# A first tile loaded in three column parts, with the parameter rows between the first and the second part

## The chip, the cores and the metric

The kernel runs on one core of one Trainium2 chip. The metric is the device time of one execution in microseconds. Ratios between kernels are the mean time of one kernel's fast runs over that of the other's fast runs of the same rounds, so they are not quite the ratio of the medians quoted beside them.

## The reference

Batch normalisation with fixed statistics over x of 32 x 256 x 128 x 128 float32:

```python
eps = 1e-5
return gamma * (x - mean) / np.sqrt(var + eps) + beta   # all four of length 256, along the channels
```

For each channel this is `x * scale + shift`. 537 MB go in and 537 MB come out; the four parameter vectors have 1 KB each.

## The kernel before

x is cut into 64 tiles of 128 partitions x 16384 columns (8.4 MB), which pass through three buffers. SP issues all loads, ACT all stores. VectorE computes columns 0 to 14335 of a tile in place, in two operations, and ScalarE the other 2048. The first tile is loaded in two halves, with the four parameter rows (each broadcast to 16 partitions) queued between them.

```python
left, right = slice(0, HW // 2), slice(HW // 2, HW)
nc.sync.dma_start(out=bufs[0][:, left], in_=xr[0][:, left]).then_inc(early, 16)
zeroed = step(nc.vector.memset(rows[:], 0.0))
for r, ap in enumerate((running_var, gamma, beta, running_mean)):
    inst = nc.sync.dma_start(out=rows[0:NE, r * C : (r + 1) * C], in_=ap.partition_broadcast(NE))
    if r == 0:
        inst._wait_ge(vec, zeroed)
    inst.then_inc(fetched, 16)
nc.sync.dma_start(out=bufs[0][:, right], in_=xr[0][:, right]).then_inc(loaded[0], 16)
for i in range(1, NT):
    s, turn = i % NBUF, i // NBUF
    if turn:
        nc.sync.wait_ge(stored[s], 16 * turn)              # the buffer is free
    inst = nc.sync.dma_start(out=bufs[s][:], in_=xr[i]).then_inc(loaded[s], 16)
    if turn:
        inst._wait_ge(vdone, 2 * (i - 1) + 1)              # VectorE is in the tile before
# ... cut: rows are transposed, scale and shift computed (VectorE, one square root on ScalarE)
vector_part(0, 0, HW // 2)._wait_ge(early, 16)
vector_part(0, HW // 2, VCOLS)._wait_ge(*landed(0))
# ... cut: vector_part for the other tiles, each waiting for landed(i)
for i in range(last):
    nc.scalar.wait_ge(vdone, 2 * (i + 1))
    inst = scalar_part(i, VCOLS)
    if i:
        inst._wait_ge(stored[(i - 1) % NBUF], 16 * ((i - 1) // NBUF + 1))
    store(i)                                               # waits for scalar_part(i)
```

## Time and profile before

| | before |
|---|---|
| median, first three runs | 2482.39 us (2482.02 to 2483.33) |
| span of the profiled run | 2483.3 us |
| bytes moved | 1073.85 MB, at a mean of 432 GB/s |
| VectorE, ScalarE busy | 20%, 6% |

The 16 DMA engines of this core are busy in all 40 slices of the profile (the prediction shows the line), at a mean of 432 GB/s. The prediction shows most of the lines. One more pair, from the timeline of the kernel before (start us, duration us, engine, line of the kernel, operation, idle time before with its releaser; SPq and ACTq in later lines are the issues of a DMA by SP and ACT):

```profile
74.26 2.09 ACT L141 ACTIVATE t<-t,shift_t,scale_t 128x2048 f32<-128x2048 f32 x1 [44.80 <-DMA out_dram<-t]
88.78 7.94 DVE L130 TENSOR_SCALAR t<-t,scale_t,shift_t 128x2560 f32<-128x2560 f32 x2 [26.45 <-DMA t<-in_x_dram]
```

At 74.26 a store has landed and the store queue is empty for a moment; at 88.78 a load has landed and the load queue is. The two moments are 14.5 us apart, so each queue has the other to fill in for it. Below this distance is called the spacing of the two gaps.

### The profile page before, as it was taken

To read this page: it belongs to the slowest core of one execution; us is meant where nothing else is said; L and a number is where in the kernel's file an instruction comes from. 1 tells how busy PE (TensorE), PEld (TensorE's weight loads), DVE (VectorE), ACT (ScalarE), POOL (GpSimd) and SP (SyncE) were. 2 spreads that over 40 slices of the span, in tenths; PEclk is the share of its full clock that TensorE was granted. 3 is DMA by queue.
4 is the path that set the end of the run, shared out by engine and by line. 5 is a ranking of instruction groups with operands and counts; after the bars stand their busy time and mean duration, and the time that the engine had idled before them with its cause. 6 is when DMAs were issued, how large, how long until landed. Compare 5 with 4: busy or idle time off the path is not lost.

```text
span 2483.3 us, 516 instructions
## 1 busy us (share of the span) xinstructions
DVE 508.8 (20%) x139; ACT 139.8 (6%) x66; POOL 0.2 (0%) x4
## 2 busy tenths in 40 slices
DVE  3122121221212212122121221212212122121220
ACT  0000000000000000000000000000000000000001
POOL 0000000000000000000000000000000000000000
DMA  9999999999999999999999999999999999999999
GB/s 415 430 439 434 428 436 436 435 433 430 432 433 438 430 432 433 435 424 437 437 428 436 438 436 429 437 435 430 436 437 436 430 437 435 429 437 435 433 433 408
DMA packets 18708, 1073.85 MB, mean 432 GB/s; under 512 B 2128, under 2 KB 2192, under 8 KB 2192
## 3 DMA queue, kind: packets, MB, share of 16 engines
q1 hardware_dynamic: 9488, 536.94, 50.1%
q10 hardware_dynamic: 9216, 536.88, 49.9%
q14 instruction: 4, 0.03, 0.0%
HBM read 536.94 MB, written 536.87 MB: 432 GB/s over the span
## 4 chain that ended last, share of the span: by engine, by line
DMA 93%; DVE 4%; another core or an unknown queue 1%; ACT 0%; issue 0%; SPq 0%; DVEq 0%
DMA t<-in_x_dram 93%; DVE t L130 4%; ACT t L141 0%; SPq L91 0%; DVE rows L89 0%; SPq L95 0%; DVE eps_t L107 0%; DVEq L198 0%; SPq L70 0%
## 5 line engine op out<-in xcount | busy, mean ns | idle before, releaser
L130 DVE TENSOR_SCALAR t<-t,scale_t,shift_t 128x11776 f32<-128x11776 f32 (+2 forms) x128 | 505.3, 3989 | 1930.4 <-DMA t<-in_x_dram 1930.2
L141 ACT ACTIVATE t<-t,shift_t,scale_t 128x2048 f32<-128x2048 f32 x64 | 138.2, 2159 | 2299.3 <-DMA out_dram<-t 2276.6
L108 DVE STREAM_TRANSPOSE turned<-rows 32x1024 f32<-32x1024 f32 x1 | 1.2, 1233 | 12.5 <-DMA rows<-in_running_mean_dram 12.5
L115 ACT ACT_TABLE_LOAD x1 | 1.3, 1283 | 0.9 <-SPq L70 0.9
L89 DVE MEMSET rows<- 32x1024 f32 x1 | 0.9, 912 | 1.2 <-SPq L70 1.2
L115 ACT ACTIVATE std_t<-par,eps_t 128x2 f32<-128x2 f32 x1 | 0.3, 296 | 14.7 <-DVE par L113 14.7
L113 DVE COPY par<-turned 32x8 f32<-32x8 f32 x4 | 0.6, 161 | 0.1
L122 DVE RECIPROCAL rstd_t<-std_t 128x2 f32<-128x2 f32 x1 | 0.2, 166 | 0.4 <-ACT std_t L115 0.4
L125 DVE TENSOR_TENSOR shift_t<-par,ms_t 128x2 f32<-128x2 f32 x1 | 0.2, 161 | 0.0
L124 DVE TENSOR_TENSOR ms_t<-par,scale_t 128x2 f32<-128x2 f32 x1 | 0.2, 161 | 0.0
L123 DVE TENSOR_TENSOR scale_t<-par,rstd_t 128x2 f32<-128x2 f32 x1 | 0.2, 160 | 0.0
L187 POOL MEMSET const-bfloat16-1.0<- 128x1 bf16 x1 | 0.1, 101 | 0.0
L187 POOL MEMSET const-uint8-127<- 128x1 uint8 x1 | 0.1, 101 | 0.0
L187 POOL MEMSET const-float32-0.0<- 128x1 f32 x1 | 0.1, 98 | 0.2 <-issue 0.2
L187 POOL MEMSET const-float32-1.0<- 128x1 f32 x1 | 0.1, 98 | 0.0
L107 DVE MEMSET eps_t<- 128x1 f32 x1 | 0.1, 59 | 0.1
## 6 DMA issues: line engine op xcount, KB each, us to landing
t<-in_x_dram SPq DMA_DIRECT2D x2, 4096.0 KB, 16.5
out_dram<-t ACTq DMA_DIRECT2D x64, 36.5
t<-in_x_dram SPq DMA_DIRECT2D x63, 37.0
rows<-in_running_var_dram SPq DMA_DIRECT2D x1, 16.0 KB, 11.3
rows<-in_gamma_dram SPq DMA_DIRECT2D x1, 16.0 KB, 11.1
rows<-in_beta_dram SPq DMA_DIRECT2D x1, 16.0 KB, 10.9
rows<-in_running_mean_dram SPq DMA_DIRECT2D x1, 16.0 KB, 11.3
```

Of the source, the lines that this page charges most:

```text
L89: zeroed = step(nc.vector.memset(rows[:], 0.0))
L107: step(nc.vector.memset(eps_t[:], eps))
L108: step(nc.vector.transpose(out=turned[:], in_=rows[:]), fetched, 16 * NPAR)
L113: placed = step(nc.vector.tensor_copy(out=flat[q * B : (q + 1) * B], in_=blocks[:, :, q, 0]))
L115: nc.scalar.activation(out=std_t[:], in_=var_t, func=mybir.ActivationFunctionType.Sqrt, bias=eps_t[:], scale=1.0,)._wait_ge(vec, placed).t ...
L122: step(nc.vector.reciprocal(out=rstd_t[:], in_=std_t[:]), act, 1)
L123: step(nc.vector.tensor_mul(out=scale_t[:], in0=gamma_t, in1=rstd_t[:]))
L124: step(nc.vector.tensor_mul(out=ms_t[:], in0=mean_t, in1=scale_t[:]))
L125: ready = step(nc.vector.tensor_sub(out=shift_t[:], in0=beta_t, in1=ms_t[:]))
L130: return nc.vector.tensor_scalar(out=t[:, first:end], in0=t[:, first:end], scalar1=scale_t[:, cb : cb + 1], scalar2=shift_t[:, cb : cb + 1 ...
L141: return nc.scalar.activation(out=t[:, first:], in_=t[:, first:], func=mybir.ActivationFunctionType.Identity, bias=shift_t[:, cb : cb + 1] ...
L187: nc = _bacc.Bacc("TRN2", target_bir_lowering=False, num_devices=1)
```

## The change

The intent is to get the parameters, and so the first elementwise operation, earlier: the rows then stand behind 0.8 MB of x instead of 4.2 MB.

```diff
+AHEAD = 1536
...
-        left, right = slice(0, HW // 2), slice(HW // 2, HW)
+        ahead, left, right = slice(0, AHEAD), slice(AHEAD, HW // 2), slice(HW // 2, HW)
...
-        nc.sync.dma_start(out=bufs[0][:, left], in_=xr[0][:, left]).then_inc(early, 16)
+        nc.sync.dma_start(out=bufs[0][:, ahead], in_=xr[0][:, ahead]).then_inc(early, 16)
         (memset of rows, the four row transfers)
+        nc.sync.dma_start(out=bufs[0][:, left], in_=xr[0][:, left]).then_inc(early, 16)
         nc.sync.dma_start(out=bufs[0][:, right], in_=xr[0][:, right]).then_inc(loaded[0], 16)
...
-        vector_part(0, 0, HW // 2)._wait_ge(early, 16)
+        vector_part(0, 0, HW // 2)._wait_ge(early, 32)
```

## The prediction

> **What bounds the kernel now.** I read four views, in this order: the page's summary, the table of stretches, the timeline of the first 30 us, and the waits of the load queue.
>
> The page (engines' busy time, then the DMA line of the 40 slices with its totals, then the chain that ended last):
>
> ```profile
> DVE 508.8 (20%) x139; ACT 139.8 (6%) x66; POOL 0.2 (0%) x4
> ...
> DMA  9999999999999999999999999999999999999999
> ...
> DMA packets 18708, 1073.85 MB, mean 432 GB/s; under 512 B 2128, under 2 KB 2192, under 8 KB 2192
> ...
> DMA 93%; DVE 4%; another core or an unknown queue 1%; ACT 0%; issue 0%; SPq 0%; DVEq 0%
> ```
>
> No compute engine is above 20%, the 16 DMA engines are full in every slice, and 93% of the chain is loads. The table of stretches (us, busy DVE, ACT, POOL, clock, DMA share, GB/s) says whether "full" holds closely:
>
> ```profile
> 0.00:30.00 30.00, 11.52 (x13) 3.67 (x3) 0.20 (x4) 1.00 0.99 411
> 30.00:100.00 70.00, 15.87 (x4) 2.09 (x1) 0.00 (x0) 1.00 0.99 423
> 100.00:500.00 400.00, 79.36 (x20) 21.64 (x11) 0.00 (x0) 1.00 1.00 434
> 2000.00:2440.00 440.00, 87.29 (x22) 25.11 (x12) 0.00 (x0) 1.00 1.00 434
> 2440.00:2478.00 38.00, 5.27 (x2) 6.36 (x1) 0.00 (x0) 1.00 1.00 433
> ```
>
> From 100 us on it holds: 433 to 434 GB/s, also in the last stretch, where loads end and stores finish alone. At 434 GB/s the 1073.85 MB take 2474 us. The span is 2483.3, so everything that start, end and slow spots cost together is 9 us. Nothing in the first tile can be worth more than a part of that 9 us; 2% would be 50 us.
>
> The timeline of the start (start us, duration us, engine, line, operation, idle time before with its releaser):
>
> ```profile
> 0.95 0.38 SPq L88 DMA_DIRECT2D t<-in_x_dram  x1
> 2.15 0.34 SPq L91 DMA_DIRECT2D rows<-in_running_var_dram  x1
> ...
> 3.46 0.43 SPq L91 DMA_DIRECT2D rows<-in_running_mean_dram  x1
> 3.93 0.44 SPq L95 DMA_DIRECT2D t<-in_x_dram  x1
> ...
> 14.79 1.23 DVE L108 STREAM_TRANSPOSE turned<-rows 32x1024 f32<-32x1024 f32 x1 [12.54 <-DMA rows<-in_running_mean_dram]
> ...
> 18.04 4.55 DVE L130 TENSOR_SCALAR t<-t,scale_t,shift_t 128x8192 f32<-128x8192 f32 x1
> 23.85 3.48 DVE L130 TENSOR_SCALAR t<-t,scale_t,shift_t 128x6144 f32<-128x6144 f32 x1 [1.27 <-DMA t<-in_x_dram]
> 27.36 2.09 ACT L141 ACTIVATE t<-t,shift_t,scale_t 128x2048 f32<-128x2048 f32 x1 [10.23 <-DVE t L130]
> 29.49 0.37 ACTq L154 DMA_DIRECT2D out_dram<-t  x1
> ```
>
> The parameter rows stand behind 4 MB of x, so the transpose starts only at 14.79, and the first elementwise operation at 18.04 instead of at about 14.05, when its half of the tile had landed (0.95 plus 13.1 to landing, by that line's issues). That 4 us is what the change aims at. But it does not reach the first store: the second VectorE operation started at 23.85 after waiting 1.27 us for the right half. The store at 29.49 hangs on that landing, not on the parameters.
>
> The load queue's own waits (for what, total us, times, longest) show the rest of the run:
>
> ```profile
> SPq L101 <- DMA out_dram<-t: 1398.1, 61, 68.8
> SPq L102 <- DVE t L130: 985.0, 61, 16.2
> ```
>
> From the fourth tile on, a load waits for a store to free its buffer and for VectorE's first part of the tile before it. These gaps cost nothing while a store is in flight, which the 434 GB/s confirms.
>
> **What the Trainium skill says.** "DMA: Bandwidth & Descriptors", section "Where 436 GB/s comes from", gives a ceiling of 435 GB/s for 16 engines; the 434 measured here is that ceiling, so only bytes or idle time can change the run. The same page, "Queues, rings and completion order", says that each DMA engine takes the descriptors of a ring in order; the trace agrees: the last row, issued at 3.46, landed 11.3 us later, behind the 4 MB, and DVE starts on it at 14.79. "Latency and other measured facts" gives about 600 ns for the first byte of a transfer issued from SP; here the first x packets appear near 1.95 us in the DMA view of the first microseconds, 1.0 us after the issue's start and 0.6 after its end at 1.33. "Anatomy of one DMA" puts most of a transfer's fixed cost of 2 us into the receipt after the last byte. Here the row packets run from about 12.1 to 13.6 us and the last row lands at 14.76, so 1.2 us after.
>
> **The change part by part.** Bytes and compute instructions stay the same. The static order of instructions of the changed kernel confirms it: one more issue on SP, all else in place.
>
> Step 1, the parameters come earlier. The first part has 128 x 1536 x 4 B = 0.79 MB, 1.8 us at 434 GB/s. It starts at 1.95, takes about 0.6 us more to ramp up (my estimate from the first packets of before, which took 1.8 us where later ones of that size took 1.2), and is out of the way at about 4.4. The last row is still issued at 3.46, reaches the engines about 1.0 us later at 4.5, and lands at about 6.3. The transpose starts there instead of at 14.79, and the scale and shift are ready 18.04 - 14.79 = 3.25 us later, at 9.6 instead of 18.04. Saved on VectorE: 8.4 us.
>
> Step 2, the DMA engines run dry for a moment. Their queue holds 9.7 us of work (4.19 MB) while SP issues the rows in the kernel before; now it holds 1.8 us. The second part is issued where the right half was, at 3.93, and reaches the engines at about 5.0. Between 4.4 and 5.0 there are only 64 packets of 1 KB. So about 0.6 us are idle or nearly so, and a second ramp of about 0.6 us follows because nothing is in flight. Against this stands what the rows cost in the kernel before, where they also thinned the stream (my sum of the packets around 12 to 14 us gives about 0.3 us lost). Net loss: 0.6 + 0.6 - 0.3 = +0.9 us on the bounding resource.
>
> Step 3, one more issue and 128 more packets. The issue of 0.44 us moves the right half and the loads of tiles 1 and 2 later, but the 3.4 MB of the second part keep the engines busy for 7.9 us meanwhile: hidden. The extra packets are 8 for each engine; I put them below 0.1 us.
>
> Step 4, the first tile. The left half is complete at about 14.05 + 0.9 = 15.0; parameters are ready long before, so VectorE starts there, 3 us earlier than 18.04, and ends at 19.5. The right half lands at 23.85 + 0.9 = 24.7, and VectorE waits some 5 us for it instead of 1.27. The 3 us turn into a longer wait. The first store goes at about 29.49 + 0.9 = 30.4. No gain here.
>
> Step 5, from there the same schedule 0.9 us later. Loads 1 and 2 (16.8 MB, 39 us) are queued already, so even the store's moment does not leave the engines idle.
>
> Sum: -0 (VectorE's gain is hidden) + 0.9 + at most 0.1 = +0.8 to +1.0 us on 2482.39, so 2483.3 us.
>
> **Rivals.**
> (a) The earlier parameters pull the first store forward and some of it reaches the end. The 4 us idle of VectorE before 18.04 speak for it; the 1.27 us wait for the right half and the full DMA engines speak against it. If the whole 1.27 us and no dry spell came through, 2481.1.
> (b) The dry spell of step 2 does not occur, since row packets and the second part arrive quickly enough, or the row packets cost less near an empty queue. Then the change is nothing but noise: 2482.4.
> (c) A changed phase between loads and stores makes their gaps coincide, and the engines idle in every tile. In the timeline the gap of the loads (88.75 to 90.42) lies 13.8 us after that of the stores (74.26 to 76.38), and both repeat each 38.6 us. A shift below 1 us is far from a collision. If it did happen, about 2 us for each of 64 tiles would make it some 2610 us, 5% slower. I give it 0.5%.
>
> **Range and chances.** The mechanisms (a) to step 2 span 2481.1 to 2483.4. Three runs of the kernel before differ by 1.3 us, and another chip may shift the level by as much again. So 2481.0 to 2485.4 should hold it 8 times in 10. A gain of 50 us isn't possible with the same bytes at the ceiling; a loss of 50 us needs (c). Faster 0.4%, within 2% 99%, slower 0.6%.
>
> **What would show each step right or wrong.** Step 1: transpose at about 6.3 us, first elementwise operation no longer released by the parameters. Step 2: a visible hole in the DMA view between 4 and 6 us, and a landing of the right half some 0.9 us later than 23.83. Step 4: VectorE's wait before its second operation grows from 1.27 to about 5 us, first store at about 30.4. Step 5: 434 GB/s between 100 and 2440 us, load spacing still 38.6 us. I am wrong if the store goes before 29.0 us and the end comes earlier by as much, if no hole appears, or if any stretch after 100 us has another rate.

## The result

| | before | changed |
|---|---|---|
| median (range), six runs each | 2482.26 us (2482.02 to 2484.1) | 2483.98 us (2483.42 to 2487.24) |
| ratio to before, 95% interval | | 1.0009 (0.9996 to 1.0022) |
| profiled span | 2483.3 us | 2481.9 us |
| parameters' transpose starts | 14.79 us | 6.23 us |
| first store issued | 29.49 us | 30.16 us |

The timeline of the changed kernel's start, columns as above:

```profile
0.95 0.38 SPq L90 DMA_DIRECT2D t<-in_x_dram  x1
...
3.92 0.42 SPq L97 DMA_DIRECT2D t<-in_x_dram  x1
...
6.23 1.23 DVE L111 STREAM_TRANSPOSE turned<-rows 32x1024 f32<-32x1024 f32 x1 [3.99 <-DMA rows<-in_running_mean_dram]
...
14.81 4.55 DVE L133 TENSOR_SCALAR t<-t,scale_t,shift_t 128x8192 f32<-128x8192 f32 x1 [5.45 <-DMA t<-in_x_dram]
24.52 3.48 DVE L133 TENSOR_SCALAR t<-t,scale_t,shift_t 128x6144 f32<-128x6144 f32 x1 [5.16 <-DMA t<-in_x_dram]
...
30.16 0.37 ACTq L157 DMA_DIRECT2D out_dram<-t  x1
```

The parameters are 8.6 us earlier and the first elementwise operation 3.2 us, now released by x and not by the rows. Then all of it is gone: VectorE waits 5.16 us for the right half instead of 1.27, starts on it 0.67 us later than before, and the first store goes 0.67 us later.

What the DMA engines did meanwhile is in the DMA view of 1.5 to 6 us (40 slices of 0.11 us; a packet's bytes count in the slice in which it starts). Before, then changed:

```profile
GB/s 0 0 0 0 2039 1748 0 291 0 583 0 0 0 0 0 0 0 0 0 291 874 1748 874 291 291 0 291 0 0 0 291 874 1456 1456 291 0 0 291 0 0
```

```profile
GB/s 0 0 0 0 437 55 218 109 55 218 55 273 109 437 382 218 546 328 546 328 546 328 546 328 546 200 374 155 137 91 956 710 1183 237 237 0 0 473 0 0
```

Before, packets of 32 KB start in bunches and each keeps its engine busy for over 1 us, so zeros between them are no idle time. In the changed kernel the packets of the first part (6 KB) start densely until 4.3 us, then come five thin slices of 200, 374, 155, 137 and 91 GB/s with the rows in them, and the second part starts only at 4.9 us. That is the hole.

Its size can be counted from the trace. I take the bytes of the load queue's packets, each spread evenly over its recorded time, divide by 435 GB/s (the stretches after 100 us hold 433 to 435), and subtract that from the time since the first packet. The rest is the time the load stream has lost. The columns count from the first packet, which starts at 1.95 us, so "3 us" is 4.95 on the timeline:

| us lost by ... after the first packet | 3 us | 5 us | 8 us | 12 us | 20 us |
|---|---|---|---|---|---|
| before | 0.86 | 0.90 | 0.92 | 1.22 | 1.32 |
| changed | 1.04 | 1.84 | 1.99 | 2.05 | 2.08 |

Before, 0.86 us go at the ramp, where the first packets take 1.85 us in the median instead of 1.21 later, and 0.30 at the rows, between 8 and 12 us. A finer count places the loss of the changed kernel on the timeline: 0.79 us by 4.5 us (before 0.85), 1.08 by 5.0 (before 0.86) and 1.85 by 7.0 (before 0.90). So the hole itself costs some 0.3 us and lies before the 3 us column. The 0.8 us between the 3 us and the 5 us column are a second ramp: the engines have packets again, but the first of these take 1.50 us in the median, where later ones of the second part take 0.99. The difference at 20 us is 0.76 us.

From there on the same schedule runs. Three lines of the changed kernel's table of stretches (columns as in the prediction), and its chain by engine:

```profile
0.00:30.00 30.00, 11.53 (x13) 3.54 (x3) 0.20 (x4) 1.00 0.94 387
...
100.00:500.00 400.00, 79.35 (x20) 20.92 (x10) 0.00 (x0) 1.00 1.00 433
...
2000.00:2440.00 440.00, 87.29 (x22) 25.11 (x12) 0.00 (x0) 1.00 1.00 434
```

```profile
DMA 92%; DVE 4%; another core or an unknown queue 2%; ACT 0%; issue 0%; SPq 0%; DVEq 0%
```

The rate differs in the first 30 us, 387 GB/s instead of 411, and the next 70 have 430 instead of 423. Packets count here where they start, which blurs the edges of a stretch; over the 100 us it is 417 against 419. The same blur stands in the last stretch, 2440 to 2478 us, with 426 against 433. In between the bound is the same.

Why then is the profiled span of the changed kernel shorter, 2481.9 against 2483.3? The timelines of before, then of the changed kernel, at the first operation on a later tile:

```profile
591.16 7.94 DVE L130 TENSOR_SCALAR t<-t,scale_t,shift_t 128x2560 f32<-128x2560 f32 x2 [30.80 <-DMA t<-in_x_dram]
630.88 7.93 DVE L130 TENSOR_SCALAR t<-t,scale_t,shift_t 128x2560 f32<-128x2560 f32 x2 [31.78 <-DMA t<-in_x_dram]
...
2448.30 5.27 DVE L130 TENSOR_SCALAR t<-t,scale_t,shift_t 128x2560 f32<-128x2560 f32 x2 [30.70 <-DMA t<-in_x_dram]
```

```profile
89.50 7.93 DVE L133 TENSOR_SCALAR t<-t,scale_t,shift_t 128x2560 f32<-128x2560 f32 x2 [26.52 <-DMA t<-in_x_dram]
...
2446.87 5.27 DVE L133 TENSOR_SCALAR t<-t,scale_t,shift_t 128x2560 f32<-128x2560 f32 x2 [31.11 <-DMA t<-in_x_dram]
```

Tile 2 comes 0.72 us later in the changed kernel (89.50 against 88.78), the last tile 1.43 us earlier. In between a tile takes 38.64 us, but some take longer: 39.72 us from 591.16 to 630.88. In the profile of before four tiles exceed 38.75 us, 2.4 us together; in that of the changed kernel one, by 0.4. In a later profile of the changed kernel it was twenty tiles and 6.3 us. These long tiles come and go between executions of one program and are larger than what the change does. Between 100 and 2440 us the three profiles lose 4.8 (before), 1.8 (changed) and 7.1 us (the later one) against 434.5 GB/s, with the engines' idle time equal within 0.1 us, so the difference is in packets that take longer; why they do is open. It is of the size of the 5 us by which single executions here differ, and no ratio below is finer than about 0.12% either way.

### The profile page after: what moved, and what is told of

It is laid out like the page before. It is cut to its first block, busy times and chain, and to the rows that moved or that the text cites. A ratio compares the mean times of both kernels' runs of the same rounds, so it can differ in the third digit from the quotient of the medians.

```text
span 2481.9 us, 517 instructions
## 1 busy us (share of the span) xinstructions
DVE 508.8 (20%) x139; ACT 139.8 (6%) x66; POOL 0.2 (0%) x4
## 4 chain that ended last, share of the span: by engine, by line
DMA 92%; DVE 4%; another core or an unknown queue 2%; ACT 0%; issue 0%; SPq 0%; DVEq 0%
DMA t<-in_x_dram 92%; DVE t L133 4%; ACT t L144 0%; SPq L93 0%; DVE rows L91 0%; SPq L97 0%; DVE eps_t L110 0%; DVEq L201 0%; SPq L71 0%
```

## The experiments

Eleven experiments ran, two of which repeat a program; all gave the reference's result. Theory: the DMA engines are full, so the change costs the hole in the load stream and gains nothing. Rivals: the split itself costs the time; an earlier first store is worth something; what matters is how the gaps of the two queues lie to each other.

Many expectations name the landing of tile 1 as the mark of a hole. That was a bad mark: by then the first store shares the engines, and it shifts between 46.0 (late10) and 57.7 us (ahead512), while the load streams differ by 2 us at most at 20 us. By this mark several expectations failed: it came at 54.56 in again, which is the changed program that had shown 55.05, at 55.64 in ahead3072 and 55.62 in split_only (54.4 to 54.5 expected, and the rival's value was 55.0), at 57.66 in ahead512 (56.2) and 52.73 in rows_act (54.3 to 54.5). The mark was given up after these results; the loss of the load stream, counted as above, took its place:

| us lost by ... after the first packet | 3 us | 5 us | 8 us | 12 us | 20 us |
|---|---|---|---|---|---|
| again (the changed kernel) | 1.05 | 1.93 | 2.03 | 2.05 | 2.08 |
| ahead512 | 2.25 | 3.05 | 3.09 | 3.15 | 3.18 |
| ahead3072, ahead3072b | 0.95, 0.91 | 1.13, 1.08 | 1.53, 1.48 | 1.59, 1.54 | 1.63, 1.58 |
| split_only | 0.85 | 0.87 | 0.94 | 1.30 | 1.44 |
| rows_act | 0.84 | 0.88 | 1.12 | 1.65 | 1.82 |
| early_store, late5 (start as before) | 0.84, 0.76 | 0.88, 0.80 | 0.89, 0.81 | 1.22, 1.15 | 1.32, 1.24 |

The last row, with the 1.32 of the kernel before itself, says how far such a figure repeats: within about 0.1 us.

### again: the changed kernel once more

No edit.

> The changed kernel once more, byte for byte the same program, for more runs on one chip beside the kernel before. Theory (a dry spell of the DMA engines of about 0.7 us in the first tile, nothing else): tile 1 lands at 55.05 again (before 54.40), and the median is 0.7 us above the kernel before, give or take what sporadic long tiles add. Rival (the change also costs something later, as the medians 2483.98 against 2482.26 suggest, 1.7 us): the difference stays at 1.5 us or more while tile 1 lands 0.65 late.

Measured: 2485.78 us median (2483.44 to 2489.0), beside 2483.53 (2482.04 to 2486.11) for before; ratio 1.0008 (0.9996 to 1.0021). The loss of 2.08 us is that of the first profile. The medians differ by 1.7 us and 2.3 us in the two sets, where the hole explains 0.8, but both intervals include no difference: whether there is more stays open. The packets give one hint, told at the end.

### ahead3072 and ahead3072b: a first part twice as long

```diff
-AHEAD = 1536
+AHEAD = 3072
```

> First part 3072 columns (1.57 MB, 3.6 us at 434 GB/s) instead of 1536, all else as changed. Theory of the dry spell: the first part ends at about 6.2 us, after the second part has reached the engines at 5.0, so the hole is gone: right half 0.6 us earlier than in the changed kernel, tile 1 lands at 54.4 to 54.5, median within 0.3 of the kernel before; parameters ready at about 11.4. Rival (splitting the transfer or its smaller packets cost the time): as slow as the changed kernel, tile 1 at 55.0.

> The 3072 column version once more, same program, for a second profile of its start and five more times. Theory: loads short by 1.6 to 1.7 us of full rate by 20 us (before 1.33, changed kernel 2.09 in two profiles), and within 0.5 us of the kernel before in the median. If the short stretch at the first store (28 to 60 us: 0.12 us lost against 1.23 and 1.27 in the changed kernel) belongs to the start and not to chance, it is near 0.12 again.

Measured: 2482.75 us beside 2483.53, ratio 0.9996 (0.9983 to 1.0008); the second time 2485.07 beside 2484.5, ratio 1.0004 (0.9992 to 1.0017). The loss is 1.6 us, so 0.5 us of the 0.76 are back, not all: of the 0.8 us between 3 and 5 us only 0.2 are left, but 0.4 us go between 5 and 8, during and after the row packets (4.4 to 5.8 us in these columns). The first expectation (no hole, tile 1 as in before within 0.1) was too bold, the second held. The timeline of ahead3072:

```profile
8.88 1.23 DVE L111 STREAM_TRANSPOSE turned<-rows 32x1024 f32<-32x1024 f32 x1 [6.63 <-DMA rows<-in_running_mean_dram]
14.48 4.55 DVE L133 TENSOR_SCALAR t<-t,scale_t,shift_t 128x8192 f32<-128x8192 f32 x1 [2.47 <-DMA t<-in_x_dram]
```

The parameters are still ready well before x. So the aim of the change can be had for 0.3 us instead of 0.76, and is no use either way.

### ahead512: a first part a third as long

```diff
-AHEAD = 1536
+AHEAD = 512
```

> First part 512 columns (0.26 MB, 0.6 us of work) instead of 1536. Theory of the dry spell: the first part ends 1.2 us earlier and the second part still comes at 5.0, so the hole is 1.2 us longer: tile 1 lands at 56.2 (changed kernel 55.05), median 1.2 us above the changed kernel. Rival (split cost): the same as the changed kernel, 55.0, since parts and packets are as many.

Measured: the loss is 3.18 us, 1.10 above the changed kernel, where 1.2 was expected; the second operation on tile 0 starts 1.03 us later than in again:

```profile
25.32 3.48 DVE L133 TENSOR_SCALAR t<-t,scale_t,shift_t 128x6144 f32<-128x6144 f32 x1 [5.16 <-DMA t<-in_x_dram]
```

The median is 2486.03 us beside 2483.53, ratio 1.0012 (0.9998 to 1.0026); it is 0.25 us above that of again, where 1.2 was expected, but the noise is larger than both. With as many parts and packets the loss grew by what the shorter first part leaves uncovered. All of the growth stands at 3 us already (2.25 against 1.05), where the longer hole is; the second ramp, from 3 to 5 us, is 0.8 to 0.9 us in both. That speaks for the hole and against the split.

### split_only: the split alone

Both left parts go before the rows.

```diff
         nc.sync.dma_start(out=bufs[0][:, ahead], ...).then_inc(early, 16)
+        nc.sync.dma_start(out=bufs[0][:, left], ...).then_inc(early, 16)
         (the rows)
-        nc.sync.dma_start(out=bufs[0][:, left], ...).then_inc(early, 16)
```

> Three parts as in the change (1536, 6656 and 8192 columns), but both left parts issued before the parameter rows, so only the split is left of the change. Theory of the dry spell: no hole, since the second part is issued 0.4 us after the first: tile 1 lands at 54.4 to 54.5, parameters late as before (transpose at about 14.8), median within 0.3 of the kernel before. Rival (split cost): tile 1 at 55.0.

Measured: 2482.82 us beside 2483.53, ratio 0.9996 (0.9983 to 1.0008). The loss is 1.44 us, 0.12 above before.

```profile
14.35 1.23 DVE L111 STREAM_TRANSPOSE turned<-rows 32x1024 f32<-32x1024 f32 x1 [12.09 <-DMA rows<-in_running_mean_dram]
...
23.58 3.48 DVE L133 TENSOR_SCALAR t<-t,scale_t,shift_t 128x6144 f32<-128x6144 f32 x1 [1.45 <-DMA t<-in_x_dram]
```

The rows are late again and the right half is early again. The split costs about 0.1 us; the rest of the 0.76 comes from where the rows stand.

### rows_act: the rows in a queue of their own

```diff
-            inst = nc.sync.dma_start(out=rows[0:NE, ...
+            inst = nc.scalar.dma_start(out=rows[0:NE, ...
```

> The kernel before (two halves) with the four rows issued from ACT instead of SP, so they have a ring of their own and SP issues the right half at once. Theory: the rows no longer stand behind 4 MB, the transpose starts at about 6 to 7 us, and the x stream has no hole: tile 1 lands at 54.3 to 54.5, median within 0.3 of the kernel before. So the aim of the change is met without its cost, and is still worth nothing in time. Rival (early parameters are worth something once the hole is gone): 1 us or more faster than the kernel before.

Measured: 2483.78 us beside 2484.37, ratio 0.9997 (0.9985 to 1.001). The time is as expected, the reason fell. Two views of rows_act, its timeline and its DMA issues (last column: us to landing):

```profile
16.36 1.23 DVE L108 STREAM_TRANSPOSE turned<-rows 32x1024 f32<-32x1024 f32 x1 [14.10 <-DMA rows<-in_running_mean_dram]
```

```profile
rows<-in_running_var_dram ACTq DMA_DIRECT2D x1, 16.0 KB, 7.5
rows<-in_gamma_dram ACTq DMA_DIRECT2D x1, 16.0 KB, 9.6
rows<-in_beta_dram ACTq DMA_DIRECT2D x1, 16.0 KB, 10.9
rows<-in_running_mean_dram ACTq DMA_DIRECT2D x1, 16.0 KB, 12.7
```

The rows came later than from behind 4 MB (16.36 against 14.79). Issued 0.5 us apart, they land about 2.2 us apart. The Trainium skill, "DMA: Bandwidth & Descriptors", section "Queues, rings and completion order", says that each engine takes turns between rings, a packet at a time. That would give this: each row has a data packet and a semaphore packet on an engine, and if each waits for one x packet of 32 KB (1.22 us), the step is 2.4 us. The time agrees; the turns themselves I did not follow engine by engine. So early parameters without a hole were not tried by this run, and its rival was not tested by it.

### early_store: the first store sooner

```diff
-            nc.scalar.wait_ge(vdone, 2 * (i + 1))
+            nc.scalar.wait_ge(vdone, 2 * (i + 1) if i else 1)
             inst = scalar_part(i, VCOLS)
+            if i == 0:
+                inst._wait_ge(*landed(0))
+                nc.scalar.wait_ge(vdone, 2)
```

A first form of it, without the wait for one VectorE part, was found to read the shift too early.

> The kernel before with ACT's part of the first tile waiting for the right half and one finished VectorE part instead of both, so it runs beside VectorE and the first store goes at about 27.4 instead of 29.5. Theory (the engines are full, the first store's moment is worth nothing): median within 0.3 of the kernel before, tile 1 lands a little later (it shares earlier), the stores land earlier. Rival (an earlier first store comes out at the end): 2 us faster.

Measured: the store goes early, as its timeline shows:

```profile
27.05 0.37 ACTq L154 DMA_DIRECT2D out_dram<-t  x1
```

The median is 2485.17 us beside 2484.37, ratio 1.0006 (0.9992 to 1.0019). A gain of 2 us would be a ratio of 0.9992, the very end of the interval; the mean is 1.5 us the other way. So an earlier first store shows no gain.

### ahead3072_early: a try at beating both

The edits of ahead3072 and early_store together.

> A try at a version that beats both: first part 3072 columns, and ACT's part of the first tile beside VectorE's, so the first store goes at about 27.7. Theory (bytes at the ceiling, nothing to gain): within 0.5 us of the kernel before, give or take the sporadic long tiles. Rival (an earlier first store shows once the parameters are early): 1.5 to 2 us faster.

Measured: 2487.73 us (four runs, 2484.46 to 2493.16) beside 2484.5, ratio 1.0016 (1.0002 to 1.0029). It beats nothing, is not within the 0.5 us expected, and is slower if anything; from four runs, one of them at 2493, I draw no cause.

### late5, late10 and wait_tile1: the first store later

In the kernel before, four or eight more transposes of the rows (late5, late10), or one wait (wait_tile1):

```diff
         step(nc.vector.transpose(out=turned[:], in_=rows[:]), fetched, 16 * NPAR)
+        for _ in range(4):          # late10: 8
+            step(nc.vector.transpose(out=turned[:], in_=rows[:]))
```

```diff
+        nc.vector.wait_ge(*landed(1))
         vector_part(0, 0, HW // 2)._wait_ge(early, 16)
```

> The kernel before with four more transposes of the rows (each 1.23 us, result unchanged), which put off the parameters by about 5 us and the first store with them: 29.5 becomes about 33.2 (the wait of 1.27 us for the right half swallows a part). Theory: the loads of tiles 1 and 2 keep the engines full until 63 us, so the end is within 0.3 of the kernel before. Rival (the first store's moment counts): 3.7 us slower.

> The kernel before with the first elementwise operation waiting until tile 1 has landed (about 43.5 us with no store beside it), so the first store goes at about 54 us, 24 us late. Theory: the store then lands after the load queue is empty (63 us), tile 3's load and tile 1's store are released by the same landing, and their gaps coincide from there on: the engines run dry once in each tile. I expect 2 to 4 us for each tile, 2600 to 2730 us, a load spacing of 41 to 43 us and 380 to 410 GB/s. Rival (the two queues drift apart again, or the gaps are covered): at most some 10 us slower, spacing back at 38.64.

> As late5 with eight extra transposes instead of four, so the first store goes about 5 us later still, near 37.6. In the eight runs so far the time from a store's landing to the next load's landing settles at about 9.7, 14.5 or 19.3 us, steps of 4.84 us, which is two packets of 2.42 us; before and after have 14.5, late5 9.7, and wait_tile1 has the two 2.4 us apart the other way and lost 3.6 us in each tile. Theory (what counts is whether the two gaps coincide, not the first store's moment): a spacing of 4.84 us here, where the gaps nearly touch; if they just miss each other the time is within 5 us of the kernel before, if they touch 20 us or more above it, and unsteady from run to run, as the one run of late5 at 2595.82 hints. Rival (the first store's moment itself counts): 7 to 8 us slower, all of it before 100 us, with 434 GB/s afterwards.

| | first store issued | spacing: store's landing to next load's landing | median | ratio to before (95%) |
|---|---|---|---|---|
| before | 29.49 us | 14.5 us | 2484.37 us (beside late5, wait_tile1) | 1 |
| late5 | 32.62 us | 9.7 us | 2487.16 us with one run at 2595.82 (slow), 2486.91 without | 1.0009 (0.9996 to 1.0023) |
| late10 | 37.77 us | 2.4 to 5.1 us | 2602.93 us with one run at 2731.79 (slow), 2600.73 without | 1.047 (1.0455 to 1.0484) |
| wait_tile1 | 52.92 us | the store lands 2.4 us after the load | 2723.94 us | 1.0964 (1.0949 to 1.0979) |

The timelines of late5, late10 and wait_tile1, each with one store's landing (start of the ACT line) and one load's (start of the DVE line):

```profile
74.82 2.10 ACT L143 ACTIVATE t<-t,shift_t,scale_t 128x2048 f32<-128x2048 f32 x1 [42.23 <-DMA out_dram<-t]
...
84.54 7.94 DVE L132 TENSOR_SCALAR t<-t,scale_t,shift_t 128x2560 f32<-128x2560 f32 x2 [25.93 <-DMA t<-in_x_dram]
```

```profile
161.46 2.09 ACT L143 ACTIVATE t<-t,shift_t,scale_t 128x2048 f32<-128x2048 f32 x1 [38.81 <-DMA out_dram<-t]
...
166.34 7.94 DVE L132 TENSOR_SCALAR t<-t,scale_t,shift_t 128x2560 f32<-128x2560 f32 x2 [33.07 <-DMA t<-in_x_dram]
```

```profile
163.78 7.94 DVE L130 TENSOR_SCALAR t<-t,scale_t,shift_t 128x2560 f32<-128x2560 f32 x2 [34.22 <-DMA t<-in_x_dram]
166.20 2.10 ACT L141 ACTIVATE t<-t,shift_t,scale_t 128x2048 f32<-128x2048 f32 x1 [40.09 <-DMA out_dram<-t]
```

And a line each of the tables of stretches of late10 and wait_tile1 (the last two figures are DMA share and GB/s):

```profile
500.00:1000.00 500.00, 95.23 (x24) 25.11 (x12) 0.00 (x0) 1.00 0.99 411
```

```profile
500.00:1000.00 500.00, 95.22 (x24) 25.14 (x12) 0.00 (x0) 1.00 0.95 396
```

Of the other versions again, ahead512, rows_act and ahead3072b keep a spacing of 14.5 us, while ahead3072, split_only, early_store and ahead3072_early settle at 19.3; in both groups one queue has work while the other has its gap, and neither is faster beyond noise. Note that ahead3072 and ahead3072b are one program: the spacing can differ between executions.

Both wait_tile1 (2600 to 2730 us) and late10 (20 us or more if the gaps touch) came out as expected, and the rate falls in all of the run, not at the start. Counted over all packets like the loss above, the engines miss 129 us in late10 and 244 us in wait_tile1, against 6 to 12 us in all other profiles (here at 434.5 GB/s): 2.0 and 3.9 us for each of some 63 tiles. A first store 8 us late costs 116 us (2600.73 - 2484.5, fast runs), one 3 us late 2.5 us, if anything. So it is not the store's moment by itself that counts; the loss goes with the spacing. Where a gap of the loads (landing, VectorE's first part, issue, first packet) meets a gap of the stores (landing, ScalarE's part, issue, first packet), neither queue has work.

That is only a part of the loss, and in late10 the smaller one: its line above has a DMA share of 0.99 at 411 GB/s, so the engines are occupied and yet move less. Counted from the packets of the tiles 3 to 61, idle engines are 0.5 of the 2.0 us lost for each tile in late10, and 2.2 of 3.9 in wait_tile1. The rest passes with a packet on every engine, but packets that take longer: in late10, after its two gaps at 163 to 165 us, the rate is 308 to 341 GB/s from 172 to 178 us with all 16 engines occupied. A 64 KB packet takes 2.42 us in the median of all these profiles; the slowest twentieth takes over 3.2 us in late10 and wait_tile1, and in before 2.42 still holds for 95 of 100. In the 39 tiles of late10 with a spacing of about 4.8 us the engines idle for 0.03 us and 1.2 us are lost all the same; in the 20 with less, 1.5 of 3.5 us are idle time. Why packets take longer after gaps that meet or nearly meet is open.

In late5 I expected a time within 0.3 us; the medians differ by 2.5 us (fast runs), in an interval that includes none, so that stays undecided. Its run at 2595.82 lies at late10's level, and late10's at 2731.79 at that of wait_tile1. Both are called slow only because they are over 1.5% above the fastest run of their kernel; the recorded clock is 1.00 in them as in all others. They may be executions whose gaps settled closer together, but they left no trace, so that is not shown.

## Why the prediction was right

The 2483.98 us (2483.3 predicted) and the range held. The time alone proves little, since 2482.4 with no hole at all would have lain in the range too; what decides are the steps:

- **The bound.** Right for this change: 433 to 435 GB/s from 100 us to 2440 in both kernels, and no version got below the time of before by more than noise. Too narrow was "only bytes or idle time can change the run": in late10 most of the loss is in packets that take longer on occupied engines.
- **Step 1, parameters.** Right: transpose at 6.23 us for 6.3.
- **Step 2, the hole.** The mechanism is shown: it stands in the DMA view at 4.3 to 4.9 us, deepens by 1.10 us with a shorter first part, and goes with a longer one. The net size was 0.76 us for 0.9. Against before, on the timeline: 0.06 less lost by 4.5 us, 0.28 more in the hole (4.5 to 5.0), 0.73 in the second ramp (5.0 to 7.0), 0.12 up to 10 us, then 0.24 saved where the rows no longer stand and 0.07 after. The prediction had put 0.6 for the hole and 0.6 for the ramp. The first part ended at 4.73 us, not at 4.4, so the hole was half as long, and the ramp cost more. That their sum of 1.2 came near 1.07 is partly luck; the 0.3 for the rows was 0.31.
- **Step 3, split.** About 0.12 us in split_only, for "below 0.1".
- **Step 4, the first tile.** Right: VectorE at 14.81 us for 15.0, a wait of 5.16 for some 5, the store at 30.16 for 30.4.
- **Step 5.** 0.72 us late at tile 2. Later the long tiles, which I had not considered beyond the spread of three runs, hide it; the two sets of runs differ by 1.7 and 2.3 us with intervals that reach 0.
- **Rival (a)**, an earlier store: not in the change (the store went later), and when forced in early_store it brought nothing. **Rival (b)**, no hole: refuted by the packets, though the time alone would not have told it. **Rival (c)**, coinciding gaps: rightly excluded for this change, since the spacing stayed at 14.5 us, and real. That its figure of 2610 us is close to late10's 2600.73 is partly luck: it meant 2 us of idle engines in each tile, and late10 has 0.5, the rest being slower packets. Its 13.8 us also does not come out of its own figures (88.75 - 74.26 is 14.5), and was too comfortable as the room to go: a first store 8 us later already uses it up.

## What to carry to other kernels

In this kernel, whose DMA engines are busy throughout, getting a small input earlier was worth nothing, because the first store did not hang on it, and an earlier first store gained nothing either: follow the wait that ends last before reordering. A short transfer at the head of a queue has to cover the issue time of what stands between it and the next large one, or the engines run dry, and starting them again cost more here (0.8 us) than the hole (0.3 us). When loads and stores take turns on the same engines, look at how far apart their gaps lie: in these profiles the spacing settles in the first tiles and stays near its value, and a store 8 us late, whose gaps meet, cost 4.7% of the run. A DMA share near 1 does not say that the rate is full: read the GB/s beside it.

## What the Trainium skill lacked or had wrong

- **Gaps of two queues that meet** (no page that I read has it): with spacings of 9.7, 14.5 or 19.3 us the time is the same within noise; at 2.4 to 5.1 us it is 4.7% longer, with the store 2.4 us behind the load 9.6%. Of the time lost in each tile, idle engines are 0.5 of 2.0 us and 2.2 of 3.9 us; the rest is in packets that take longer (cause open). The steps between the settled spacings are 4.84 us, which is two packets of 64 KB (2.42 us each in the trace); that the turns of the two rings set this grid is my inference.
- **"DMA: Bandwidth & Descriptors", "Queues, rings and completion order"**: it gives 9 to 17 descriptors as typical for a packet, the unit of taking turns. Here the 16 KB rows landed 2.2 us apart beside a stream of 32 KB descriptors (rows_act), which fits turns of one descriptor each (an inference, not followed on single engines). A small transfer in a second ring beside a large one is not quick: 7.5 to 12.7 us to landing.
- **"HBM Reference", "Specifications (TRN2)"**: it gives about 425 GB/s for a core streaming alone; here 433 to 435 GB/s hold for over 2300 us, read and write together.
- **Starting again after a hole** (no page that I read has it): the first packets of the second part took 1.50 us in the median where later ones took 0.99 (changed kernel), and 0.8 us of full rate were lost in the 2 us after the hole; at the start of the kernel before it was 1.85 us for 1.21.
- **Long tiles** (no page that I read has it): single tiles of 38.8 to 39.9 us among tiles of 38.64, 0.4 to 6.3 us in a profile; the engines are not idle in them, the packets take longer; cause open.
- **The first store's arrival** (no page that I read has it): between 28 and 60 us the engines lose 1.14 to 1.27 us in the changed kernel and ahead512 (three profiles), 0.44 to 0.87 where the load stream starts as before (five), 0.12 to 0.22 with 3072 columns (three). It repeats among these, and would add some 0.4 us to the change's 0.76; but split_only has 0.39 and rows_act, with the two halves of before, 0.12, so it does not follow from the parts alone. Its cause is open.
